# A two-layer GLA and SSD backbone whose scheduler orders every queue by its other machine model

## The chip, the cores and the metric

The program runs on one core of a Trainium2 chip. The core has a matrix engine (TensorE, PE in the profile, its weight loads PEld), a vector engine (DVE), a scalar engine (ACT), GpSimd (POOL) and SyncE (SP), which here issues all DMAs. Each engine takes its instructions from a queue of its own, in the order in which they stand there, and waits for others by semaphores. The metric is the device time of one execution in microseconds. Before the change the median of three runs is 1954.72 us.

## The reference, cut to what matters

Two layers of a diffusion backbone on 512 latent tokens and 256 context tokens, model width 1024. Layer 0 mixes tokens by bidirectional gated linear attention (GLA, 4 heads), layer 1 by a bidirectional Mamba-2 scan (SSD, 8 groups); each is followed by a squared-ReLU MLP of width 4096, and every sub-layer by a LayerNorm with residual.

```python
for i in range(DEPTH):                       # DEPTH = 2
    m_l = split((s_lat @ ada_w[i] + ada_b[i]), 6)      # shifts, scales, gates, for latent tokens
    m_c = split(s_ctx @ ada_w[i] + ada_b[i], 6)        # and for context tokens
    ul, uc = snake(modulate(hl, m_l[0], m_l[1])), modulate(hc, m_c[0], m_c[1])
    yc, yl = gla_mixer(uc, ul, ...) if i == 0 else ssd_mixer(uc, ul, ...)
    hl = layer_norm(ALPHA * hl + m_l[2] * snake(yl), ...)
    hl = layer_norm(ALPHA * hl + m_l[5] * sq_relu_mlp(modulate(hl, m_l[3], m_l[4]), w1, w2), ...)
    ...                                      # the same for hc, while it is needed

def step(s, inp):                            # one chunk of the SSD scan
    cum = jnp.cumsum(dti * a, axis=1)
    decay = jnp.exp(jnp.where(mask, cum[:, :, None] - cum[:, None, :], -jnp.inf))
    y = einsum('bijg,bijgr,bjgrp->bigrp', einsum('bign,bjgn->bijg', ci, bi), decay, xdt)
    y = y + einsum('bign,bigr,bgrpn->bigrp', ci, exp(cum), s)
    s_new = s * exp(cum[:, -1:]) + einsum('bjgn,bjgr,bjgrp->bgrpn', bi, exp(last - cum), xdt)
```

## The kernel before, in words

Activations lie transposed, channels on partitions and the 768 tokens along the free axis, in eight tiles of 128 channels. Every large product is done in three parts: a weight tile and an activation tile are each split into a rounded high part and a rest (`wh`, `wl`: L203 on ACT, L204 on DVE; `xh`, `xl` likewise), and `prod` (L231 to L240) issues for each of its K tiles the matmuls wh with xh, wh with xl and wl with xh, for 512 latent and, where needed, 256 context columns. These L240 rows, with their relatives L520 in the GLA projections, are called the main matmuls. A weight block passes through `raw` (4 buffers), `wh` and `wl` (3 each). Products have 4 PSUM banks of their own (`mm`), and everything else shares the 4 others (`sm`).

The small work of a layer is written as Python generators. `worked` counts the columns of the main matmuls and, for each 768 of them, may take one step of the queue `side` (a GLA head's scan, an SSD group's scan, a LayerNorm) and every few steps one of `background` (rows of the adaLN products, L157). So the program's text already lays side work among main matmuls; `drain` finishes what is left of `side` at fixed points.

That text is not yet the order. The Tile framework takes it as a priority: it goes through the program with a model of the machine, and puts on each engine's queue next what the model says can start first, with the text's order where several can. What the model believes of durations thus decides where a side row stands among the main matmuls, and where a side row of ACT, DVE or POOL stands among the others of its engine. The semaphores are set after that.

The places that the text below speaks of:

- SSD group (`group`, `conv`, `inner`): `conv` copies a product to `pre`, applies five taps (L865 on ACT, four L867 on DVE) and a gate (L869, L870), giving `cf`. `inner` transposes B and x to `Bn` and `xnat` (L877 on PE, evacuated by L878 on ACT), weights x by the decay to `xw` (L931 on DVE), forms chunk states (L943, L946 on PE), chains them to the states `ST` (L931 and L951 on DVE), forms C by B (L963, copied by L965), the part from the states (L986 on PE; L987 and L989 on DVE, L988 on POOL) and the part within a chunk (L1009 on PE, added by L1012 on DVE). The decays inside a chunk are tiles `L`, two for each of four chunks: loaded by DMA (L910), masked on POOL (L912), exponentiated on ACT (L998), summed in pairs on POOL (L1001), multiplied by C by B on DVE (L1002), and read by L1009. There are 7 buffers for L (`LB`); L1001 frees one of a pair, L1009 the other. L1031 to L1037 finish the group.
- GLA head (`scan`): seven levels, each with exponentials E (L602, L603), products (L604 on DVE), running sums W (L612 to L615) and scores (L574 on PE); then the keys are scaled (L626, L627) and transposed (L637, evacuated by L638), chunk states formed (L645) and stepped (L658), outputs made (L676), normalised (L678 to L681) and transposed back (L703).
- LayerNorm (`layer_norm`): transposes to tokens (L304 on PE), statistics (L305 to L312), the normalised tile `xn` (L315 on ACT), transposes back (L325 on PE), evacuation with gains (L353 on ACT, L355 on DVE). L147 is a SiLU on ACT for the adaLN rows of the next layer.

## Time and profile before

| | before |
|---|---|
| time, median of three runs (lowest, highest) | 1954.72 us (1950.36, 1959.47) |
| the profiled execution, by its span | 1959.6 us |
| mean granted TensorE clock | 0.990 |
| start and layer 0 (GLA), 0 to 400 us | PE busy 50.10 of the first 60 us, 326.63 of the next 340 |
| FFN of layer 0, 452 to 940 us | PE busy 484.00 of 488 |
| dt block and first convolutions, 940 to 1050 us | PE busy 104.25 of 110 |
| SSD tail and norm, 1476 to 1600 us | PE busy 119.05 of 124 |
| FFN of layer 1 and last norm, 1600 to 1959.6 us | PE busy 348.76 of 359.6 |

For the profiled execution the page gives its span and no other time. The span counts from the first to the last instruction of the core; busy time of an engine is the union of its instructions, so overlapped matmuls aren't counted twice there, while the sums of a group of lines can overlap. A bracket behind a row of the timeline, such as [3.25 <-DVE xw L931], is idle time just before that row and what ended it. PEclk and the column behind POOL in the window rows are the share of full speed that TensorE's clock was granted.

### The profile page before, as it was taken

The numbers are of one execution on the slowest core, as the hardware profiler recorded it, in microseconds if no ns is written. First come the engines' busy times: TensorE is split into PE (matmuls) and PEld (weight loads), VectorE is DVE, ScalarE is ACT, GpSimd is POOL, SyncE is SP. The second block draws the span as 40 slices with busy tenths as digits, with TensorE's granted clock in tenths as the row PEclk, the third lists the DMA queues.
The fourth block names the chain that finished last, engine by engine and source line by source line (L and its number), as shares of the span: only waits on it lengthen the run. The fifth ranks groups of instructions, "written<-read, shape, count | busy, mean of one in ns | idle before, by whom it ended". The sixth has DMA issues, their size and how long they took to land.

```text
span 1959.6 us, 29026 instructions
## 1 busy us (share of the span) xinstructions
PE 1881.3 (96%) x11405; PEld 1604.9 (82%) x11405; DVE 1254.9 (64%) x1929; ACT 798.6 (41%) x1386; POOL 410.8 (21%) x448
## 2 busy tenths in 40 slices
PE   7999999999999999999999999999999999999997
PEld 5988888788788888888897787777877788888886
DVE  4798887888655444324578888777887673333345
ACT  3445456454113123122366555455543353323231
POOL 2134242202002002010104432333321321102012
PEclk9999999999999999999999999999999999999999
DMA  8423313214444444313134433333434523333331
GB/s 329 156 73 114 104 36 106 65 55 150 141 142 140 138 137 135 116 41 116 33 107 121 129 115 112 104 101 129 121 100 132 164 73 105 96 99 96 96 89 54
DMA packets 78936, 219.01 MB, mean 112 GB/s; under 512 B 11056, under 2 KB 15792, under 8 KB 78800
## 3 DMA queue, kind: packets, MB, share of 16 engines
q1 hardware_dynamic: 78800, 217.17, 35.1%
q8 instruction: 89, 1.46, 0.3%
q14 instruction: 47, 0.39, 0.1%
HBM read 209.01 MB, written 8.13 MB: 111 GB/s over the span
## 4 chain that ended last, share of the span: by engine, by line
PE 63%; DVE 13%; DMA 7%; ACT 6%; POOL 5%; issue 5%; SPq 0%; DVEq 0%; POOLq 0%; ACTq 0%
PE mm L240 54%; DMA L<-crowc 4%; POOL L L1001 1%; ACT L L998 1%; DMA raw<-in_ada_wr_dram 1%; DVE A L593 1%; PE sm L943 1%; DVE raw L157 1%; DVE cv L867 1%; POOL L L912 1%; PE sm L676 1%; DVE wl L204 1%; POOL W L612 1%; PE sm L986 1%; PE mm L520 1%
## 5 line engine op out<-in xcount | busy, mean ns | idle before, releaser
L240 PE MATMUL mm<-xh,wh 128*128 128x512 f32 (+1 forms) x1824 | 554.2, 357 | 2.8 <-ACT xh L1044 2.6
L240 PE MATMUL mm<-xl,wh 128*128 128x512 f32 (+1 forms) x1824 | 550.0, 354 | 1.5 <-DVE xl L1045 1.5
L240 PE MATMUL mm<-xh,wl 128*128 128x512 f32 (+1 forms) x1824 | 549.7, 353 | 1.4 <-DVE wl L204 1.4
L203 ACT CAST wh<-raw 128x1024 fp32r<-128x1024 f32 (+3 forms) x227 | 227.8, 1004 | 658.5 <-PE mm L240 617.3
L204 DVE TENSOR_TENSOR wl<-raw,wh 128x1024 fp32r<-128x1024 f32 (+3 forms) x227 | 275.6, 1215 | 173.6 <-ACT wh L203 170.1
L240 PEld LDWEIGHTS mm<-xh,wh 128*128 128x128 f32 x1824 | 304.4, 189 | 54.4 <-ACT xh L1044 3.8
L240 PEld LDWEIGHTS mm<-xl,wh 128*128 128x128 f32 x1824 | 303.7, 189 | 50.6 <-issue 3.1
L240 PEld LDWEIGHTS mm<-xh,wl 128*128 128x128 f32 x1824 | 303.5, 189 | 50.7 <-DVE wl L204 2.5
L385 POOL TENSOR_TENSOR rq<-rr 128x768 f32<-128x768 f32 (+1 forms) x62 | 104.6, 1687 | 684.7 <-ACT rr L384 648.4
L240 PE MATMUL mm<-rl,wh 128*128 128x512 f32 x704 | 212.5, 355 | 3.8 <-DVE rl L387 3.8
L240 PE MATMUL mm<-rh,wl 128*128 128x512 f32 x704 | 212.4, 355 | 0.0
L240 PE MATMUL mm<-rh,wh 128*128 128x512 f32 x704 | 212.1, 355 | 0.0
L419 DVE SCALAR_TENSOR_TENSOR acc<-mm,row,acc 128x256 f32<-128x256 f32 (+1 forms) x182 | 100.7, 580 | 150.4 <-PE mm L240 150.0
L157 DVE SCALAR_TENSOR_TENSOR raw<-raw,srow 128x1024 f32<-128x1024 f32 x104 | 131.6, 1268 | 83.0 <-DMA raw<-in_ada_wr_dram 81.8
L867 DVE SCALAR_TENSOR_TENSOR cv<-pre,cvec,cv 128x770 f32<-128x770 f32 (+1 forms) x128 | 135.2, 1057 | 14.9 <-ACT cv L865 11.9
L240 PEld LDWEIGHTS mm<-rl,wh 128*128 128x128 f32 x704 | 116.0, 189 | 23.8 <-DVE rl L387 4.2
L240 PEld LDWEIGHTS mm<-rh,wh 128*128 128x128 f32 x704 | 116.1, 189 | 19.6
L240 PEld LDWEIGHTS mm<-rh,wl 128*128 128x128 f32 x704 | 116.1, 189 | 19.6
L998 ACT ACTIVATE L<-L,lcol 128x128 f32<-128x128 f32 x256 | 81.9, 393 | 69.1 <-POOL L L912 69.1
L387 DVE TENSOR_TENSOR rl<-rq,rh 128x768 fp32r<-128x768 f32 (+2 forms) x67 | 53.2, 794 | 64.0 <-POOL rq L385 63.7
L912 POOL TENSOR_SCALAR_AFFINE_SELECT L<-L 128x512 f32<-128x512 f32 x64 | 52.2, 817 | 142.5 <-DMA L<-crowc 141.4
L869 ACT ACTIVATE cf<-cv 128x512 f32<-128x512 f32 (+1 forms) x56 | 27.6, 533 | 86.5 <-DVE cv L867 86.5
(290 smaller groups left out, 2513.0 us busy)
## 6 DMA issues: line engine op xcount, KB each, us to landing
raw<-in_ffn_w_dram SPq DMA_DIRECT2D x112, 512.0 KB, 3.8
raw<-in_ada_wr_dram SPq DMA_DIRECT2D x80, 512.0 KB, 3.7
raw<-in_ssd_w_in_dram SPq DMA_DIRECT2D x48, 512.0 KB, 3.9
L<-crowc SPq DMA_DIRECT2D x64, 256.0 KB, 3.8
raw<-in_ada_w_dram SPq DMA_DIRECT2D x16, 512.0 KB, 9.1
raw<-in_gla_w_in_dram SPq DMA_DIRECT2D x16, 512.0 KB, 3.7
ec<-crow SPq DMA_DIRECT2D x64, 128.0 KB, 3.0
acc<-in_xT_dram SPq DMA_DIRECT2D x14, 384.0 KB, 6.9
```

Source lines behind the costliest of these rows:

```text
L157: nc.vector.scalar_tensor_tensor(o, raw, 1.0, srow[s], ALU.mult, ALU.mult, accum_out=t[:, b, s:s + 1])
L203: nc.scalar.copy(h, src)
L204: nc.vector.tensor_sub(l, src, h.bitcast(F32))
L240: nc.tensor.matmul(part_of(ps, t0, n), a[:, k, :], b[:, t0:t0 + n], start=(k == 0 and i == 0), stop=(k == kt - 1 and i == 2))
L385: eng.tensor_mul(q[:, a:b], r[:, a:b], r[:, a:b])
L387: nc.vector.tensor_sub(rl[:, a:b], q[:, a:b], rh[:, a:b].bitcast(F32))
L419: nc.vector.scalar_tensor_tensor(acc[m][:, t0:t0 + n], part_of(ps, t0, n), gate[:, m, s:s + 1], (src or acc)[m][:, t0:t0 + n], ALU.mult, A ...
L520: nc.tensor.matmul(ps[:, 256 * tt:256 * tt + 256], a, b, start=(k == 0 and i == 0), stop=(k == KT - 1 and i == 2))
L867: nc.vector.scalar_tensor_tensor(c[:, 0:n], pre[:, t:t + n], cw(t), c[:, 0:n], ALU.mult, ALU.add)
L869: nc.scalar.activation(f[:, t0:t1], c[:, t0 + d:t1 + d], AF.Tanh)
L912: nc.gpsimd.affine_select(out=L[z], in_=L[z], compare_op=ALU.is_ge, fill=NEG, base=0, pattern=[[0, 4], [1 - 2 * z, P]], channel_multiplier ...
L998: nc.scalar.activation(t[:, h, :], t[:, h, :], AF.Exp, bias=lcol[:, c, r:r + 1])
```

## The change

One argument where the program is built asks the scheduler to use its other machine model, TimelineSim, in place of its default one. The other lines of the diff blank comments.

```diff
-    with _tile.TileContext(nc) as tc:
+    with _tile.TileContext(nc, schedule_with_timeline_sim=True) as tc:
         tile_backbone(tc, *args)
```

The instructions and their operands are the same on PE, DVE, POOL and SP. ACT gets six table loads more, all in the GLA scan, because exponentials and other functions alternate there more often. The main matmuls keep their order among themselves nearly everywhere; what moves is the side work. Three places follow.

The first is SSD group 4 of 0 to 7. On PE, around the first chunk states, before (names: `mm` a product's bank, `sm` a bank of the shared four, wh_12051 the weights of a convolution's product):

```order
L240 MATMUL mm_12055<-xh_8666,wl_12052 128x512
L240 MATMUL mm_12056<-xh_8666,wl_12052 128x256
L943 MATMUL sm_12151<-xw_12135,Bn_12069 128x512
L943 MATMUL sm_12153<-xw_12138,Bn_12069 128x512
L963 MATMUL sm_12162<-cf_11720,cf_11642 128x128 x4
L240 MATMUL mm_12055<-xh_8668,wh_12051 128x512
L240 MATMUL mm_12056<-xh_8668,wh_12051 128x256
L946 MATMUL sm_12171<-xw_12159,Bn_12069 128x256 x2
```

The same rows of PE now:

```order
L240 MATMUL mm_12309<-xh_8660,wh_12304 128x256
L943 MATMUL sm_12151<-xw_12135,Bn_12069 128x512
L240 MATMUL mm_12308<-xl_8661,wh_12304 128x512
L240 MATMUL mm_12309<-xl_8661,wh_12304 128x256
L943 MATMUL sm_12153<-xw_12138,Bn_12069 128x512
L963 MATMUL sm_12162<-cf_11720,cf_11642 128x128 x4
L946 MATMUL sm_12171<-xw_12159,Bn_12069 128x256 x2
```

They stand two weight blocks later, among the products of wh_12304 in place of wh_12051. The transposes ahead of them (L877) have moved later too, and the four L1009 of the group before, which stood 4.7 us of main matmuls apart, now stand close together.

On DVE, in the same group, the end of the state chain before, from the last `xw` on:

```order
L931 TENSOR_TENSOR xw_12181<-xnat_12070,wc 128x256
L931 TENSOR_TENSOR ST_12133<-ST_12132,dtot 128x256
L931 TENSOR_TENSOR ST_12132<-ST_12133,dtot 128x256
L951 TENSOR_TENSOR ST_12133<-ST_12133,sm_12188 128x256
L1002 TENSOR_TENSOR L_12201<-L_12201,cbs_12167 128x512
L951 TENSOR_TENSOR ST_12132<-ST_12132,sm_12190 128x256
L931 TENSOR_TENSOR ST_12134<-ST_12133,dtot 128x256
L931 TENSOR_TENSOR ST_12131<-ST_12132,dtot 128x256
L951 TENSOR_TENSOR ST_12134<-ST_12134,sm_12190 128x256
L951 TENSOR_TENSOR ST_12131<-ST_12131,sm_12188 128x256
```

And the first half of that piece of DVE's queue now, again from the last `xw` on:

```order
L931 TENSOR_TENSOR xw_12181<-xnat_12070,wc 128x256 x2
L867 SCALAR_TENSOR_TENSOR cv_12212<-pre_12211,cvec,cv_12212 128x770
L931 TENSOR_TENSOR ST_12132<-ST_12131,dtot 128x256
L1002 TENSOR_TENSOR L_12201<-L_12201,cbs_12167 128x512
L1002 TENSOR_TENSOR L_12332<-L_12332,cbs_12167 128x512
L1002 TENSOR_TENSOR L_12386<-L_12386,cbs_12167 128x512
L1002 TENSOR_TENSOR L_12465<-L_12465,cbs_12167 128x512
L951 TENSOR_TENSOR ST_12134<-ST_12134,sm_12151 128x256
L951 TENSOR_TENSOR ST_12132<-ST_12132,sm_12171 128x256
L870 SCALAR_TENSOR_TENSOR cf_12213<-cf_12213,cv_12212 128x512
L870 SCALAR_TENSOR_TENSOR cf_12213<-cf_12213,cv_12212 128x256
```

Between these and the last L951 of the group follow five more L931, five more L951, one L204 and three L867 of 512 columns.

The second place is the end of GLA head 2 on PE. Before, the last two scores and the first transposes of keys stood apart, with main matmuls between, as in this piece:

```order
L637 MATMUL sm_3011<-ident,W_2478 128x128 x4
L240 MATMUL mm_2947<-xh_111,wl_2952 128x512
L240 MATMUL mm_2948<-xh_111,wl_2952 128x256
L240 MATMUL mm_2947<-xh_113,wh_2951 128x512
L240 MATMUL mm_2948<-xh_113,wh_2951 128x256
L637 MATMUL sm_3021<-ident,W_2478 128x128 x4
L240 MATMUL mm_2947<-xl_114,wh_2951 128x512
```

Now PE has them in one block, which goes on through L645, L676 and L703 without a main matmul:

```order
L240 MATMUL mm_3272<-xh_3230,wl_3268 128x256
L574 MATMUL sm_2918<-E_2838 64x64 x12
L574 MATMUL sm_2968<-E_2898 64x64 x12
L637 MATMUL sm_3001<-ident,W_2478 128x128 x4
L637 MATMUL sm_3011<-ident,W_2478 128x128 x4
L637 MATMUL sm_3021<-ident,W_2478 128x128 x4
L645 MATMUL sm_3033<-v_1693,kn_3000 128x256 x2
```

The third is the LayerNorm behind the GLA mixer, on ACT, where one segment's last evacuation (L353) is followed by the next one's `xn` (L315). Before:

```order
L353 ACTIVATE lnu_4244<-sm_4239,l00B,l00G 128x256
L203 CAST xh_3993<-lnu_4226 128x256
L353 ACTIVATE lnu_4249<-sm_4239,l00B,l00G 128x256
L315 ACTIVATE xn_4281<-sm_4263,lnrs_4277 128x512
L315 ACTIVATE xn_4281<-sm_4269,lnrs_4277 128x512
```

Now on ACT:

```order
L353 ACTIVATE lnu_4244<-sm_4239,l00B,l00G 128x256
L147 ACT_TABLE_LOAD
L147 ACTIVATE srow_4597<-srow_4597 128x1024
L203 CAST xh_3993<-lnu_4226 128x256
L147 ACTIVATE srow_4598<-srow_4598 128x1024
L353 ACTIVATE lnu_4249<-sm_4239,l00B,l00G 128x256
L203 CAST xh_3995<-lnu_4244 128x256
L315 ACTIVATE xn_4281<-sm_4263,lnrs_4277 128x512
```

The table load and the two SiLU rows, which stood one segment later, have moved ahead of the last evacuation and of the next `xn`. On PE the sixteen L304 and the sixteen L325 of that segment now follow one another without a main matmul between.

## The prediction, made before the changed kernel was run

> **What bounds the kernel now.** The first view is the page's head and its chain, for what the end hangs on.

> ```profile
> span 1959.6 us, 29026 instructions
> PE 1881.3 (96%) x11405; PEld 1604.9 (82%) x11405; DVE 1254.9 (64%) x1929; ACT 798.6 (41%) x1386; POOL 410.8 (21%) x448
> PE mm L240 54%; DMA L<-crowc 4%; POOL L L1001 1%; ACT L L998 1%; DMA raw<-in_ada_wr_dram 1%; DVE A L593 1%; PE sm L943 1%; DVE raw L157 1%; DVE cv L867 1%; POOL L L912 1%; PE sm L676 1%; DVE wl L204 1%; POOL W L612 1%; PE sm L986 1%; PE mm L520 1%
> ```

> TensorE is busy for 1881.3 us, so no order can gain more than the other 78 plus what busy time hides of a halved clock. The chain's second item, the loads of the L tiles, says where the order matters: in the SSD groups. Hence the second view, busy time by stage (span, then PE busy, PE weight loads, DVE, ACT, POOL, then clock).

> ```profile
> 60.00:400.00 340.00, 326.63 (x2585) 288.21 (x2584) 283.72 (x418) 174.39 (x274) 94.77 (x89) 1.00 0.29 91
> 400.00:452.00 52.00, 48.77 (x381) 46.75 (x380) 43.97 (x110) 31.91 (x64) 3.29 (x6) 0.97 0.17 52
> 1050.00:1476.00 426.00, 399.77 (x2215) 323.29 (x2215) 348.71 (x518) 229.71 (x492) 145.12 (x190) 0.98 0.36 113
> 1650.00:1850.00 200.00, 200.00 (x884) 165.60 (x883) 71.95 (x74) 56.58 (x69) 25.44 (x16) 1.00 0.31 97
> ...
> PE sm L943 <- DVE xw L931: 15.4, 9, 3.6
> PE sm L877 <- ACT Bn L878: 7.5, 4, 2.9
> PE sm L877 <- DVE cf L870: 3.3, 1, 3.3
> ```

> The last window row is pure FFN, without idle: 200/884 = 0.226 us for a matmul of 512 columns, the rate by which I count cover below. Seven SSD groups (1050 to 1476, 61 us each) leave TensorE idle for 26.2 us, and the lower rows, its waits there, account for all of it. DVE is busy for 348.71 of 426 us, 82%. The clock is 0.98 there; these windows show why:

> ```profile
> 1181.30:1184.70 3.40, 3.40 (x9) 2.09 (x9) 2.53 (x8) 0.70 (x3) 0.64 (x1) 0.50 0.27 67
> 1242.70:1246.10 3.40, 3.40 (x8) 1.81 (x7) 2.40 (x8) 0.49 (x2) 0.63 (x1) 0.50 0.29 70
> 1180.63 3.12 PE L943 MATMUL sm<-xw,Bn 128*128 128x512 f32 x4 [2.11 <-DVE xw L931]
> ```

> After a wait TensorE ran for 3.4 us at half clock, which costs 1.7 us; 426 x (1 - 0.98) = 8.5 us is five of these. The last row shows one behind a wait of only 2.11 us. [...]

> **What the wait in a group hangs on** (the timeline of group 4, five engines):

> ```profile
> 1221.90 0.66 PE L1009 MATMUL sm<-L,xnat 128*64 128x128 f32 x8
> 1233.92 0.87 PE L877 MATMUL sm<-ident,cf 128*128 128x128 f32 x6 [0.50 <-ACT Bn L878]
> 1232.18 1.29 POOL L1001 TENSOR_TENSOR L<-L,L 128x512 f32<-128x512 f32 x1
> 1233.50 0.32 SPq L910 DMA_DIRECT2D L<-crowc  x1
> 1238.76 1.28 ACT L998 ACTIVATE L<-L,lcol 128x128 f32<-128x128 f32 x4 [3.87 <-POOL L L912]
> 1239.94 0.83 ACT L878 COPY xnat<-sm 128x512 f32<-128x512 f32 x2
> 1240.80 2.60 DVE L931 TENSOR_TENSOR xw<-xnat,wc 128x256 f32<-128x256 f32 x6 [6.16 <-ACT xnat L878]
> 1242.21 3.25 PE L943 MATMUL sm<-xw,Bn 128*128 128x512 f32 x4 [3.25 <-DVE xw L931]
> ```

> L943 waits for xw, xw for L878; L878's input, of the L877 at 1233.92, was there at 1235, but ahead of it on ACT stands L998, which waits for a tile of L, whose DMA waits for a buffer that L1001 frees. That chain begins with the last L1009 of the group before and takes 20 us; the order covers it with 13.2 us of main matmuls and some 3 of other rows.

> **The change part by part.** Counts and work stay; only positions move, besides six table loads on ACT (1.28 us each, in the GLA scan), which ACT at 174 of 340 us there hides; uncovered they would be 8 us.

> *SSD, first L943.* Main matmuls from the last L1009 of one group to the first L943 of the next: before 13.2 us in groups 1 to 6, after 17.6 to 24.4. So far the wait of 3.25 is covered. But the four L1009 of a group, spread over 14 us before, now stand within 3 to 5 us, so more of the loads begin only there. From the first L1009 the cover was 27.5 us and is 21.9 to 27.6: nothing gained. Bounds: all 26.2 us go, or none. In groups 3, 5 and 6 L878 still stands behind the seventh prefetched tile's L998, in 1, 2 and 4 one tile less. I take two thirds, **-17**, and half of the clock loss, **-4**.

> *SSD, L986.* It needs the state chain ST (L931, L951), which the old order keeps together on DVE and the new one mixes with other work.

> ```profile
> L867 DVE SCALAR_TENSOR_TENSOR cv<-pre,cvec,cv 128x770 f32<-128x770 f32 x88 | 100.9, 1146 | 11.0 <-ACT cv L865 8.3 <-POOL L L1001 1.2
> L204 DVE TENSOR_TENSOR wl<-raw,wh 128x1024 fp32r<-128x1024 f32 x42 | 57.6, 1372 | 8.7 <-ACT wh L203 8.6
> L951 DVE TENSOR_TENSOR ST<-ST,sm 128x256 f32<-128x256 f32 x56 | 22.0, 410 | 3.6 <-PE sm L946 2.0 <-PE sm L943 1.5
> L867 DVE SCALAR_TENSOR_TENSOR cv<-pre,cvec,cv 128x512 f32<-128x512 f32 x28 | 21.7, 776 | 0.0
> L870 DVE SCALAR_TENSOR_TENSOR cf<-cf,cv 128x512 f32<-128x512 f32 x30 | 21.1, 704 | 5.3 <-ACT cf L869 5.3
> L870 DVE SCALAR_TENSOR_TENSOR cf<-cf,cv 128x256 f32<-128x256 f32 x23 | 20.5, 892 | 0.0
> L1002 DVE TENSOR_TENSOR L<-L,cbs 128x512 f32<-128x512 f32 x28 | 18.9, 679 | 0.0
> L931 DVE TENSOR_TENSOR ST<-ST,dtot 128x256 f32<-128x256 f32 x42 | 18.8, 472 | 0.0
> ...
> L943 PE MATMUL sm<-xw,Bn 128*128 128x512 f32 x56 | 31.0, 666 | 15.6 <-DVE xw L931 15.4
> L986 PE MATMUL sm<-cf,ST 128*128 128x128 f32 x224 | 29.7, 275 | 0.5 <-DVE ST L951 0.4
> ```

> Group 4, from the last xw to the last ST. Before, on DVE: 4 x 0.47 + 4 x 0.41 + 0.68 = 4.2 us; TensorE from the last L943 to the second L986 tile 4.0, and 0.4 us of wait is all that the last row shows for seven groups. After: seven L951 (2.9), six L931 (2.8), four L1002 (2.7), L867 1.15 + 3 x 0.78, L870 0.70 + 0.89 and L204 1.37, together 14.8 us; TensorE has 10.0 of main matmuls, one L943 row (31.0/28 = 1.1) and four L986 rows (29.7/112 = 0.27 each), 12.2. The excess is 2.6 us; worked so, the eight groups give 0.8 to 3.3, in all about 14, **+13** after taking off the excess that before shows without a wait. Below: 0, if DVE runs ahead of TensorE (it idles 18% here); above: 25, with halved clock behind each.

> *GLA scan.* Its waits:

> ```profile
> PE sm L574 <- DVE E L604: 5.3, 8, 1.7
> PE sm L637 <- DVE W L627: 2.6, 3, 0.9
> PE sm L676 <- DVE W L658: 2.0, 2, 1.6
> ```

> Inside the heads these rows now stand up to 23 us of main matmuls later: -7 of these 9.9. At the end of head 2, though, everything from the last but one L574 to L703 is one block; before, 76 main matmuls, 38 pairs x 1.5 x 0.226 = 12.9 us, lay between. That cover is the upper end for the stall, the lower is the 2 us or so that stand there now: I take +8 and 1.7 for the clock. Heads 1 and 3 lose part of theirs, +3. Sum **+6** (-6 to +14).

> *LayerNorm at 400 to 452.*

> ```profile
> L315 ACT ACTIVATE xn<-sm,lnrs 128x512 f32<-128x512 f32 x12 | 8.8, 775 | 14.3 <-DVE lnrs L312 14.3
> L147 ACT ACTIVATE srow<-srow 128x1024 f32<-128x1024 f32 x2 | 2.1, 1069 | 0.0
> L147 ACT ACT_TABLE_LOAD x1 | 1.3, 1283 | 0.0
> ```

> The table load and both L147 (3.4 us) move ahead of the last L353 and the next L315; sixteen L304 and sixteen L325 stand behind one another, so TensorE waits for both: between 0 and 3.4 plus a third of L315's 14.3 (there are three token segments), 8 us; I take **+5**. The start and the other norms shift by little: **+1** (0 to 3).

> Sum: -17 - 4 + 13 + 6 + 5 + 1 = **+4** on the profiled 1959.6. That execution is 4.9 above the median of the runs shown (1954.72); carried over, 1958.7, rounded to 1958.

> **Rivals.** *All waits in SSD go.* For it: the cover from the last L1009 grows by 4 to 11 us where 3.25 lack, and DVE has 18% free, so that it may be ahead at L986. Against it: the crowded L1009. With 6 left at L986 it gives -26 - 8.5 + 6 + 6 + 5 + 1 = -17, about 1938, and 1925 if the GLA ends cost little too.

> *DVE becomes the bound of every group* (slower). Place: the DVE queue between L943 and L986. 348.71/7 = 49.8 us of DVE stand against 399.77/7 = 57.1 of TensorE; when TensorE's idle shrinks, DVE has 7 us a group for all its own waits, of which the view shows 30 us for L878 alone. If the first L943 still comes over 3 us early in most groups, its waits and clock stay and the L986 waits come on top, 13 and four half-clock windows of 1.7, 20 in all: 0 + 0 + 20 + 6 + 5 + 1 = +32, about 1987. It decides as soon as L943 waits as long as now. Rows above speak for it: L870 takes 892 ns on 256 columns and 704 on 512, so something slows DVE. [...]

> *The order hardly differs in effect:* 1955. The rows of the order speak against it.

> **How the numbers follow.** About 0.5% is what a measurement of this kernel can tell from no change: 1945 to 1964.5. The forecast 1958 has 0.37, the order without effect 0.03, together 0.40 within that bound; all waits gone 0.27 (faster); DVE as the bound, or the GLA and norm costs at their upper ends with SSD as now, 0.33 (slower). Lower ends: -26 - 8.5 + 0 - 6 + 5 + 1 = -35, or 1920; upper: the +32 of 1987; leaving a tenth at each side gives 1925 to 1985.

> **What would show it.** In SSD: waits of L943 on xw down to about 9 us, new waits of L986 on ST of about 13, fewer half-clock windows. In GLA: one idle stretch of 8 us or more with L637, L676 and L703 in it near the end of head 2. At the norm: L304 or L325 waiting for ACT for about 5 us more. I am wrong about the L tiles if L943 waits as before or not at all, and about DVE if L986 doesn't wait.

## The result: 83 us slower, and the profile after

| | before | after |
|---|---|---|
| time, median of four runs (lowest, highest) | 1955.60 us (1950.36, 1959.47) | 2038.84 us (2036.54, 2045.56) |
| ratio, 95% interval | | 1.042 (1.0388 to 1.0452) |
| span of the profiled execution | 1959.6 us | 2034.6 us |
| mean granted TensorE clock | 0.990 | 0.978 |

The head of the page after, to be read against that of before:

```profile
span 2034.6 us, 29053 instructions
PE 1906.8 (94%) x11405; PEld 1624.1 (80%) x11405; DVE 1269.8 (62%) x1929; ACT 806.2 (40%) x1392; POOL 405.7 (20%) x448
```

The span is 75.0 us longer, TensorE's busy time 25.5, so the other 49.5 us are idle time. Lower clock can make at most 17 of the 25.5: by the clock records TensorE is busy for 62.5 us of its half-clock time after and for 28.7 before, and half clock costs at most half of that. Another 6.4 us lie in the FFN of layer 0, which is no slower in clock (last section). To see where the rest lies, I cut both executions at the same main matmuls, counted along TensorE's queue; a stage is then the same main work, though side work may have moved across a cut. The cuts lie where the execution before is at 59, 395, 480, 940, 1050, 1476 and 1600 us. "Half" is time at half clock (granted share 0.50); it costs at most half of what TensorE is busy in it. All stages are those of one execution of each kernel.

| stage (us) | before | after | difference | idle, before to after | half, before to after |
|---|---|---|---|---|---|
| start | 58.8 | 60.2 | +1.4 | 9.9 to 11.1 | 0 to 0 |
| GLA scan, heads 0 to 2 | 336.2 | 347.3 | +11.1 | 13.3 to 27.3 | 0 to 23.9 |
| head 3, output product, LayerNorm | 85.0 | 123.7 | +38.7 | 3.4 to 23.0 | 3.4 to 23.9 |
| FFN of layer 0 | 460.0 | 466.9 | +6.9 | 3.8 to 4.3 | 6.8 to 3.4 |
| its norm, dt block | 111.0 | 121.0 | +10.0 | 6.2 to 13.7 | 0 to 3.4 |
| SSD groups | 425.0 | 424.9 | -0.1 | 25.9 to 27.2 | 17.1 to 17.1 |
| SSD tail | 124.2 | 128.5 | +4.3 | 4.8 to 7.1 | 2.6 to 5.2 |
| FFN of layer 1, last norm | 359.3 | 362.2 | +2.9 | 10.9 to 14.1 | 7.7 to 10.6 |

Fifty of the 75 us lie in layer 0's mixer and its LayerNorm, and 33.6 of these are idle time (16.7 before, 50.3 after). The busy time there (the first two rows are about this stage, before and after, the third is the SSD stretch after) and three half-clock windows after:

```profile
60.00:480.00 420.00, 403.24 (x3128) 359.22 (x3127) 351.63 (x560) 217.81 (x354) 106.59 (x99) 1.00 0.29 91
61.50:531.30 469.80, 420.46 (x3136) 371.06 (x3137) 374.00 (x577) 229.60 (x363) 105.31 (x105) 0.95 0.27 85
1116.00:1545.00 429.00, 401.77 (x2233) 326.84 (x2232) 345.46 (x523) 227.46 (x483) 139.60 (x187) 0.98 0.37 114
...
319.00:336.10 17.10, 11.42 (x73) 9.62 (x74) 12.69 (x20) 7.21 (x10) 1.65 (x2) 0.50 0.36 117
428.20:438.40 10.20, 7.42 (x32) 6.51 (x32) 5.76 (x8) 4.29 (x7) 0.82 (x2) 0.50 0.48 161
462.30:476.00 13.70, 7.31 (x33) 6.50 (x34) 6.83 (x20) 10.61 (x20) 1.10 (x2) 0.50 0.00 1
```

TensorE ran at half clock for 17.1, 10.2 and 13.7 us in one piece: at the end of head 2, at the end of head 3, in the LayerNorm. Before, no piece was longer than 6.8 us ahead of the last norm. TensorE was busy for 26.1 of the 41 us, so half clock cost at most 13 us of them. The first and the third piece fall into blocks of side rows, but for a few us: after, such blocks stand on TensorE from 319.3 to 350.4 (31.1 us) and from 457.5 to 474.4 (16.9 us), while before the longest such block of this stage takes 9.0 us. TensorE's timeline after at the start of the first block:

```profile
319.34 1.55 PE L574 MATMUL sm<-E 128*64 128x64 f32 x24 [1.65 <-DVE E L604]
324.50 1.55 PE L574 MATMUL sm<-E 128*64 128x64 f32 x24 [3.61 <-DVE E L604]
327.10 2.79 PE L637 MATMUL sm<-ident,W 128*128 128x128 f32 x12 [1.05 <-DVE W L627]
330.57 6.40 PE L645 MATMUL sm<-v,kn 128*128 128x256 f32 x16 [0.68 <-ACT kn L638]
```

The same 24 L574 take 0.92 us at full clock and 1.55 here. The waits of these rows come to 7.0 us; what stands between and behind them runs at half clock until 336.1. In the LayerNorm, on TensorE and ACT:

```profile
461.75 1.28 ACT L147 ACT_TABLE_LOAD   x1
463.04 1.06 ACT L147 ACTIVATE srow<-srow 128x1024 f32<-128x1024 f32 x1
464.00 0.39 ACT L203 CAST xh<-lnu 128x256 fp32r<-128x256 f32 x1
464.30 1.05 ACT L147 ACTIVATE srow<-srow 128x1024 f32<-128x1024 f32 x1
465.26 0.55 ACT L353 ACTIVATE lnu<-sm,l00B,l00G 128x256 f32<-128x256 f32 x1
...
466.53 1.09 PE L304 MATMUL sm<-ident,acc 128*128 128x128 f32 x4 [3.34 <-DVE acc L355]
471.10 3.25 PE L325 MATMUL sm<-ident,xn 128*128 128x128 f32 x14 [3.06 <-ACT xn L315]
```

L304 gets its bank when the evacuation behind the table load and the two SiLU rows is done (L355 on DVE empties the bank from 465.84 to 466.38, just after L353 on ACT), and L325 then waits for the statistics and `xn`, with no main matmul between.

At the end of head 3 the wait of L703 is the longest of the stage:

```profile
424.48 1.04 ACT L203 CAST wh<-raw 128x1024 fp32r<-128x1024 f32 x1 [2.56 <-DMA raw<-in_ffn_w_dram]
425.43 0.38 ACT L678 ACTIVATE on<-sm 128x256 f32<-128x256 f32 x1
...
428.03 0.36 PE L703 MATMUL sm<-ident,on 128*128 128x128 f32 x1 [4.41 <-ACT on L681]
```

The last L676 ended at 423.6, but on ACT an L203 of the FFN's weights, itself waiting for their load, stood ahead of the L678 that normalises the head's output, so L678 began 1.8 us later.

In the SSD groups the waits have other names and the same sum, as TensorE's list of waits there shows:

```profile
PE sm L877 <- DVE cf L870: 9.3, 6, 4.2
PE mm L240 <- ACT pre L857: 6.4, 2, 3.5
PE sm L943 <- DVE xw L931: 4.9, 3, 2.0
PE sm L943 <- DVE ST L931: 2.5, 1, 2.5
PE sm L986 <- DVE ST L951: 1.8, 1, 1.8
```

L943's wait for xw is down from 15.4 us and L877's for Bn is gone; in their place stand waits for the convolutions (L870) and for L857, which empties a product's bank. An example of the latter from the timeline, at the first group:

```profile
1111.79 1.28 ACT L998 ACTIVATE L<-L,lcol 128x128 f32<-128x128 f32 x4 [3.46 <-POOL L L912]
1112.98 0.61 ACT L869 ACTIVATE cf<-cv 128x512 f32<-128x512 f32 x1
1113.50 0.56 ACT L857 COPY pre<-mm 128x512 f32<-128x512 f32 x1
...
1114.11 0.88 PE L240 MATMUL mm<-xh,wh 128*128 128x512 f32 x2 [4.45 <-ACT pre L857]
```

It is the old mechanism with another victim: an L998 that waits for a tile of L stands ahead of the row that TensorE needs. The same stands ahead of both L857 waits inside the groups (3.54 and 2.90 us, with L998 waiting 3.19 and 4.97 us) and of the longest L870 wait (4.24 us, with L998 waiting 3.60 us ahead of the L869 that L870 needs). The shorter L870 waits were not traced back.

### The profile page after: what moved, and what is told of

It is laid out like the page before. It is cut to its first block, busy times and chain, and to the rows that moved or that the text cites. A ratio compares the mean times of both kernels' runs of the same rounds, so it can differ in the third digit from the quotient of the medians.

```text
span 2034.6 us, 29053 instructions
## 1 busy us (share of the span) xinstructions
PE 1906.8 (94%) x11405; PEld 1624.1 (80%) x11405; DVE 1269.8 (62%) x1929; ACT 806.2 (40%) x1392; POOL 405.7 (20%) x448
## 5 line engine op out<-in xcount | busy, mean ns | idle before, releaser
L240 PE MATMUL mm<-xh,wh 128*128 128x512 f32 (+1 forms) x1824 | 562.1, 359 | 20.5 <-ACT pre L857 14.5
L240 PE MATMUL mm<-xl,wh 128*128 128x512 f32 (+1 forms) x1824 | 561.0, 357 | 7.3 <-DVE xl L204 5.9
L240 PE MATMUL mm<-xh,wl 128*128 128x512 f32 (+1 forms) x1824 | 558.5, 355 | 0.4 <-DVE wl L204 0.4
L203 ACT CAST wh<-raw 128x1024 fp32r<-128x1024 f32 (+3 forms) x227 | 226.9, 1003 | 669.5 <-PE mm L240 650.5
L204 DVE TENSOR_TENSOR wl<-raw,wh 128x1024 fp32r<-128x1024 f32 (+3 forms) x227 | 276.7, 1221 | 183.3 <-ACT wh L203 178.3
L240 PEld LDWEIGHTS mm<-xh,wh 128*128 128x128 f32 x1824 | 308.7, 191 | 75.4 <-ACT pre L857 16.2
L240 PEld LDWEIGHTS mm<-xl,wh 128*128 128x128 f32 x1824 | 310.0, 191 | 60.4 <-DVE xl L204 8.5
L240 PEld LDWEIGHTS mm<-xh,wl 128*128 128x128 f32 x1824 | 308.3, 190 | 50.8 <-issue 4.3
L240 PE MATMUL mm<-rl,wh 128*128 128x512 f32 (+1 forms) x704 | 214.5, 356 | 4.3 <-DVE rl L387 4.2
L240 PE MATMUL mm<-rh,wh 128*128 128x512 f32 x704 | 215.6, 360 | 0.0
L240 PE MATMUL mm<-rh,wl 128*128 128x512 f32 (+1 forms) x704 | 213.6, 357 | 0.0
L157 DVE SCALAR_TENSOR_TENSOR raw<-raw,srow 128x1024 f32<-128x1024 f32 x104 | 135.4, 1304 | 117.7 <-DMA raw<-in_ada_wr_dram 116.7
L867 DVE SCALAR_TENSOR_TENSOR cv<-pre,cvec,cv 128x770 f32<-128x770 f32 (+1 forms) x128 | 134.4, 1050 | 18.3 <-ACT cv L865 16.8
L240 PEld LDWEIGHTS mm<-rl,wh 128*128 128x128 f32 x704 | 118.0, 189 | 26.1 <-DVE rl L387 4.9
L240 PEld LDWEIGHTS mm<-rh,wh 128*128 128x128 f32 x704 | 117.2, 189 | 19.3
L240 PEld LDWEIGHTS mm<-rh,wl 128*128 128x128 f32 x704 | 116.4, 189 | 19.8
L998 ACT ACTIVATE L<-L,lcol 128x128 f32<-128x128 f32 x256 | 82.2, 393 | 82.2 <-POOL L L912 82.2
L912 POOL TENSOR_SCALAR_AFFINE_SELECT L<-L 128x512 f32<-128x512 f32 x64 | 60.2, 942 | 139.5 <-DMA L<-crowc 110.1
L870 DVE SCALAR_TENSOR_TENSOR cf<-cf,cv 128x512 f32<-128x512 f32 (+1 forms) x56 | 40.4, 751 | 28.8 <-ACT cf L869 28.6
```

What stands on the lines that cost most here:

```text
L157: nc.vector.scalar_tensor_tensor(o, raw, 1.0, srow[s], ALU.mult, ALU.mult, accum_out=t[:, b, s:s + 1])
L203: nc.scalar.copy(h, src)
L204: nc.vector.tensor_sub(l, src, h.bitcast(F32))
L240: nc.tensor.matmul(part_of(ps, t0, n), a[:, k, :], b[:, t0:t0 + n], start=(k == 0 and i == 0), stop=(k == kt - 1 and i == 2))
L867: nc.vector.scalar_tensor_tensor(c[:, 0:n], pre[:, t:t + n], cw(t), c[:, 0:n], ALU.mult, ALU.add)
L870: nc.vector.scalar_tensor_tensor(f[:, t0:t1], f[:, t0:t1], 1.0, c[:, t0 + d:t1 + d], ALU.add, ALU.mult)
```

## Experiments

All differences below are between medians: each kernel against the runs of the kernel before that were taken with it. The kernel after stands at +83.2 us (76 to 88 by its interval). Code is shortened: NoSync stands for a dependency that only fixes the order.

**TensorE in the text's order.** The kernel after; at its end each TensorE instruction of a stage is tied behind the one before it in the program's text (an edge of order only, without a semaphore):

```diff
+ins = [i for i in nc.cur_bb.bb.instructions[a:b] if i.engine == PE]
+for p, q in zip(ins, ins[1:]):
+    tc.add_manual_dep(q, p.name, NoSync, reason="text order")
```

> The kernel after, with one addition: on TensorE the instructions of the GLA scan and of the LayerNorm behind it stand in the text's order (each is tied to the one before it on its queue); all else is ordered by the new model. Theory A (TensorE's own order makes the loss: side rows in blocks without main matmuls, which cost idle time and then halved clock): 35 to 50 us of the 83 come back, about 1990 to 2005. Rival B (ACT's, DVE's and POOL's order makes the rows late wherever they stand): within 10 us of the kernel after, the waits only move to other rows.

> As the run before, but only the GLA scan's TensorE rows are tied to the text's order; the LayerNorm keeps its block of 32 transposes. Theory A: 25 to 35 us come back, and the LayerNorm still shows halved clock and some 10 us of idle. Rival B: within 10 us of the kernel after.

> The other part: only the LayerNorm's TensorE rows are tied to the text's order, the GLA scan keeps the new order with its blocks at the ends of heads 2 and 3. Theory A: 12 to 18 us come back, and this and the run before add up to the first. Rival B: within 5 us of the kernel after.

> Only the SSD groups' TensorE rows are tied to the text's order; everything before them is as in the kernel after. If the new order costs next to nothing there (waits moved, not added), the time is within 8 us of the kernel after. If the SSD groups hold a part of the loss that the comparison by stages hides, it is over 15 us lower; if the new order is good there, over 15 higher.

Measured: +61.7 (GLA and LayerNorm), +71.2 (GLA alone), +75.5 (LayerNorm alone), so 22, 12 and 8 us back, about half of what I expected; and +175.2 with the SSD groups tied, 92 worse than after. The blocks were gone, but the first part of the scan was now slower than in either kernel (262 us from 59 to a cut at 300, against 244 before and 236 after), and the SSD stage stood idle for 74 us. The text's order isn't the order that the default model makes: it, too, had moved side rows later to where their inputs are ready. These runs don't decide between the theories.

**The old order, engine by engine.** The next kernels build the program a second time with the other model, read each engine's order from that, and tie the instructions of one stage to it:

```diff
+with _tile.TileContext(dry) as tc:           # or with the new model
+    tile_backbone(tc, *dargs)
+pos = order_of(dry)
 with _tile.TileContext(nc, schedule_with_timeline_sim=True) as tc:
     tile_backbone(tc, *args)
+    pin(nc, tc, pos, [PE, DVE, Activation, Pool, SP], start_of_stage, end_of_stage)
```

> The kernel after, but in the GLA scan, its output product and the LayerNorm behind it every engine's queue (TensorE, DVE, ACT, POOL, SP) stands in the order of before, each instruction tied to the one before it; from the FFN of layer 0 on all is ordered by the new model. Theory A (the orders of this stage together make the 50 us): 44 to 52 us less than after, about 1990, with GLA and LayerNorm at 421 to 427 us as before. Rival B (the stage is slow for another reason, such as where buffers lie): less than 15 us back.

> The reverse: the kernel before, ordered by the default model, with the order of after on all five engines in the same stage only. Theory A: 44 to 52 us more than before, about 2005. Rival C (the loss comes of both halves, the stage's order and what the rest prefetches): 10 to 30 us more.

Measured: +47.4, so 36 us back, and +36.5 in the reverse. Both are under what I expected, but they agree: the stage's order makes 36 us of the loss, whatever orders the rest. In the profile the scan is as before (92.2 us between the cuts at 300 and 395); head 3 and LayerNorm take 94.1, 9 us more than before though their own order is the old one, so that much of their 38.7 comes from outside this stage's order (the FFN's order right behind it is tried below).

> The kernel after with TensorE alone in the order of before in that stage; the model places the other engines' work around it. Theory A1 (TensorE's blocks are the cause; the others' order follows from it): 40 us or more back, about 1995. Theory A2 (an engine's order fits only the orders of the others; the loss is in the mixture): clearly less, as with the text's order on TensorE (17 us back).

> The complement: DVE, ACT, POOL and SP in the order of before in that stage, TensorE placed by the new model. Theory A1: TensorE's blocks remain, under 15 us back. If the late rows are made by ACT and DVE (tables, LayerNorm's SiLU rows ahead): over 30 us back. A2: something between, or worse than after.

Measured: +62.9 and +74.8, so 20 and 8 us back, against 36 for both together: as A2 says, an engine's order is worth less without the others'. With TensorE's old order among the others' new ones, the first part of the scan takes 261 us.

> The kernel before with TensorE alone in the new order, in the GLA scan alone; the default model places the other engines' work around it. If TensorE's blocks at the ends of heads 2 and 3 suffice for the loss of the scan (28 us with all five engines in the new order): 20 us or more above before, with the long half-clock stretch there. If the other engines' order makes it: under 12 us.

Measured: +28.3, as much as with all five engines. In this direction TensorE's order suffices to make a loss of this size. That the block makes it is not shown by this run: its half-clock stretch of 17.1 us (305.8 to 322.9) lies ahead of the block (321.3 to 345.0), where main matmuls wait for ACT and DVE (1.37 us for `xh`, 1.24 and 5.72 for `xl`), and in the block no wait is longer than 1.11 us. With TensorE's order alone the loss is as large, but other rows are late.

> The kernel before with the new order, on all five engines, in the GLA scan alone (the output product and the LayerNorm behind it keep the old order). If the ends of heads 2 and 3 carry the loss: 18 to 30 us more than before, with two half-clock stretches of 10 us or more. If it is the LayerNorm: under 10 us more.

> The kernel before with the new order in the GLA output product and the LayerNorm behind it alone. By the difference to the run of the whole stage: 8 to 18 us more than before, with the table load and both SiLU rows ahead of the evacuation and one half-clock stretch of 7 us or more. If head ends carry it: under 8 us more.

Measured: +28.0 and +11.0, both in the expected range; their sum, 39, is the 36.5 of the whole stage within the spread of the runs. One thing expected of the first did not come: of two half-clock stretches of 10 us or more only the one at the end of head 2 is there (17.1 us). At the end of head 3 its profile has two single windows of 3.4 us and no L703 wait above 1.0 us, so the 4.41 us wait and the 10.2 us stretch of the kernel after are not made by the scan's order alone.

> The kernel after with the old order on all five engines in the SSD layer (from its dt block to its output product), the new one elsewhere. If the new order costs nothing net in the groups but 10 us at their start and 3 at the tail: 10 to 18 us less than after. If the groups hold more of the loss: over 25 less. If the new order gains there: no less than after.

> The kernel after with the old order on all five engines in the FFN of layer 0 and the LayerNorm behind it, the new one elsewhere. By the stages, what lies between the first LayerNorm and the SSD groups costs some 20 us beyond that LayerNorm's own order (about 10 where the FFN's first products follow the norm, about 10 at the second norm and the dt block): if the FFN stage's order makes them, 15 to 22 us less than after; if they come of the order on either side of it, under 8 us.

Measured: +66.1 and +60.6, so 17 and 23 us back; by their intervals, with the kernel after held at +83.2, 6 to 21 and 12 to 31. By the stages the old FFN order gives 9 us at the first norm and 3 at the second, and its FFN itself is 8.5 us shorter, which the last section leaves open. For the SSD layer the profile, of the slowest of its four runs, shows only 3 of the 17, so where they lie is not shown; of the 10 us at the second norm and dt block, neither run gives back more than 3. With 36 for the first stage the three parts make 76 of the 83 by medians, 67 without the FFN's 8.5. The start, and everything from the SSD layer's output product on, were not tried; by the table that is 1.4 and 2.9 us and a part of the SSD tail's 4.3.

**The wait of before, taken away.** The kernel before, with one tie on ACT: the L998 of a group stand behind the last L878 of the group ahead.

```diff
-    nc.scalar.activation(t[:, h, :], t[:, h, :], AF.Exp, bias=lcol[:, c, r:r + 1])
+    behind(tc, nc.scalar.activation(t[:, h, :], t[:, h, :], AF.Exp, bias=lcol[:, c, r:r + 1]), g)
...
+def behind(tc, op, g):                       # NATS: the L878 in text order, six for a group
+    if g:
+        tc.add_manual_dep(op.ins, NATS[6 * g - 1].ins.name, NoSync)
```

> The kernel before, with one tie on ACT in the SSD groups: the L998 of a group stand behind the last L878 of the group ahead of it, no longer before it. Theory (the wait of L943 for xw, and of L877 for Bn, is L878 queued behind an L998 that waits for the DMA of its tile L): these waits, 22.9 us, and half of the clock loss of 8.5 go, 15 to 30 us less than before. Rival (the chain from L877 to L943 is itself too long for its cover, or the prefetch of L comes too late for L1009 then): within 8 us of before, with the wait moved to L986 or L1009.

Measured: 1937.78 us, 23.7 less than before; ratio 0.9901 (0.9869 to 0.9933). TensorE's waits and busy time in the SSD groups:

```profile
PE sm L877 <- DVE cf L870: 3.1, 1, 3.1
PE mm L240 <- ACT xh L1044: 2.6, 1, 2.6
PE sm L1009 <- issue: 2.5, 1, 2.5
PE sm L986 <- DVE ST L951: 1.4, 4, 0.4
PE sm L943 <- DVE xw L931: 0.7, 4, 0.2
...
1050.00:1460.00 410.00, 401.72 (x2241) 326.27 (x2242) 360.15 (x527) 234.83 (x499) 153.31 (x190) 0.99 0.39 124
```

L943's wait falls from 15.4 to 0.7 us and L877's for Bn, 7.5 us, is gone. The SSD stage takes 401.9 us in place of 425.0, with 8.1 us idle in place of 25.9 and 6.0 at half clock in place of 17.1. So the reading of before was right: an L998 that waits for its tile stood in front of L878. The rival's signs are small: L986 waits 1.4 us and L1009 2.5. This version is faster than both kernels.

## Why the prediction was wrong, point by point

It said 1958 us, within 1925 to 1985, most likely no measurable change. It was 2038.84. The sum of the parts was +4 and should have been +83.

The step that failed is the one from moved rows to time in layer 0 and at the norms: it credited waits that stayed, took the clock behind a block at one window, and put places whose rows were not counted at next to nothing.

- *GLA scan, +6 (-6 to +14): measured +28.* This is the largest error. In the kernel with only the scan's order new, idle time from the start of the scan to the FFN rises by 16.5 us, where the sum has -7 + 8 + 3 = 4. The -7 for waits inside the heads did not come: up to the cut at 300 TensorE is idle for 12.7 us, against 10.5 before (after: 12.8). The stall at the end of head 2 was taken at 8 us; its waits come to 8.7 after (5.3 for E, 1.1 for W, 1.0, 0.7 and 0.6 for the rest), and between the cuts at 300 and 395 idle time rises by 11.7 in all. The clock behind it was taken at one window, 1.7 us; it was five, 17.1 us. TensorE was busy for 11.4 of them, so this cost at most 5.7.
- *LayerNorm, +5: measured +11* for its own order, and some 9 more in the kernel after, with the FFN's new order behind it. The mechanism, both waits one after the other, was right (3.34 and 3.06 us in the rows above); the 13.7 us at half clock had no term, and as TensorE was busy for 7.3 of them they cost at most 3.7.
- *First L943 in the SSD groups, -17, and clock, -4.* The waits named did fall, from 22.9 us for xw and Bn to 4.9, as the longer cover says. But waits for L870 and L857 took their place, 15.7 us where before had 3.3, and the groups end where they did. The prediction had the tiles of L as what delays ACT, and asked only who waits for L878; it didn't ask whom else on ACT the same L998 would hold up.
- *L986, +13: measured 1.8* (4.3 with L943's wait for ST). DVE was ahead of TensorE when the state chain began: its last `xw` ended 1.1 to 5.5 us before TensorE's last L943 or L946 of the group, against 1.2 to 1.3 us before the change; this was named as the lower end. For group 4 alone the working gave 2.6 us, and there the wait is 1.83. The rival that DVE becomes the bound of every group needed L943 to wait as long as before, and it waits 4.9 us in place of 15.4. Nor does a busier DVE bind: with the tie on ACT it is busy for 360.15 of 410 us, 88%, and TensorE waits for it for some 6 us in all.
- *Start and other norms, +1 (0 to 3): measured some 19* from the table: 1.4 at the start, 10.0 at the second norm and the dt block, 4.3 at the SSD tail, 2.9 at the last FFN and norm. The prediction gave no rows for "shift by little". At the second norm and the dt block TensorE waits for L857 alone 8.1 us after, 4.45 of them behind the L998 shown above.

The FFN of layer 0, 6.9 us longer, had no term at all. The rival that came nearest in time, 1987, had the wrong place. Idle time and clock couldn't be priced apart here: in the block of short rows at the end of head 2, without main matmuls between, a window with 0.68 us of idle time was still followed by one at half clock (last section).

## What to carry to other kernels

When small work moves into one block on TensorE, count the main matmuls left between its rows, not only how late each row's input is: in the block at the end of head 2, which has none for 31.1 us, waits of 0.68 to 3.61 us came to 7.0 us, and a half-clock piece of 17.1 us fell on it. An order fits the other engines' orders: with the better order on TensorE alone, 16 of 36 us stayed lost here. And when a row on an engine waits for a transfer, ask for every row behind it who needs it: tying such rows, the L998 of each group, behind the rows that don't wait was worth 24 us here (13 to 26 by the interval), while the other machine model as a whole cost 83.

## What the runs showed of the hardware

The halved clock (granted share 0.50) came in multiples of 3.4 us: 3.4, 6.8, 10.2, 13.7 and 17.1 us in these profiles, apart from the last piece, which the end of the program cuts off. The window ahead of the longest piece after, and its five windows:

```profile
315.60:319.00 3.40, 0.98 (x4) 0.60 (x4) 3.40 (x3) 0.00 (x0) 0.24 (x1) 1.00 0.10 21
319.00:322.40 3.40, 1.55 (x24) 1.39 (x24) 3.28 (x7) 1.69 (x2) 1.54 (x2) 0.50 0.28 102
322.40:325.80 3.40, 1.30 (x24) 1.33 (x24) 3.37 (x5) 1.91 (x3) 0.11 (x1) 0.50 0.00 0
325.80:329.20 3.40, 2.35 (x15) 2.19 (x13) 2.94 (x3) 2.56 (x4) 0.00 (x0) 0.50 0.00 0
329.20:332.60 3.40, 2.72 (x9) 1.96 (x8) 0.53 (x1) 1.05 (x2) 0.00 (x0) 0.50 0.50 147
332.60:336.00 3.40, 3.40 (x10) 2.65 (x9) 2.56 (x6) 0.00 (x0) 0.00 (x0) 0.50 0.98 329
```

Ahead of the piece TensorE was idle for 2.4 us of a window, in two waits (1.30 and 1.65 us), neither of which is long. Inside it the window with 0.68 us of idle time was followed by another at half clock, and the first window without any by full clock. All changes of the clock in a profile lie on one grid of 3.413 us, to 0.01 us.

The FFN of layer 0 took either 457 to 460 or 465 to 469 us (463 in one profile), with about as little idle time and half clock in the one as in the other (3.8 us idle and 6.8 at half clock before, 4.3 and 3.4 after). A stretch of it before and after is an example (main matmuls in the same order, 0.176 us each as against 0.173):

```profile
640.00:840.00 200.00, 200.00 (x1156) 174.83 (x1155) 85.85 (x117) 39.78 (x51) 15.92 (x9) 1.00 0.41 126
692.50:896.30 203.80, 203.69 (x1155) 176.73 (x1154) 89.22 (x122) 39.75 (x51) 16.42 (x9) 1.00 0.40 129
```

Kernels with the old order in the FFN were found at both: 466.5 us with the new order in the LayerNorm alone, 458.4 with the old order in the FFN alone; of seven profiles with it four lie at 457 to 460 and three at 465 to 468. All nine with the new order took 463 us or more. So the old order doesn't keep the FFN from the slower time; whether the new one helps to bring it on, and what makes it, stays open.
